# Five groups of seven in four blocks of the first gate/up products, and earlier accumulating transfers in the second's

## The chip, the cores and the metric

The kernel runs on one core of one Trainium2 chip. The core has five engines with instruction queues of their own: TensorE (PE in the profile; its weight loads are shown as PEld), VectorE (DVE), ScalarE (ACT), GpSimd (POOL) and SyncE (SP, which here only issues transfers). Sixteen DMA engines move data between the chip's memory and the core's on-chip memory. The metric is the device time of one execution in microseconds (us); less is better.

## The reference

One decoder layer in float32, on 256 tokens of 2048 features, with DeepNorm residuals:

```python
h = layer_norm(alpha * h + 0.5 * swiglu(h, w_ffn1_gu[i], w_ffn1_down[i]), ln_g[i, 0], ln_b[i, 0])
...
mixed = (jax.nn.sigmoid(gate_r) * ret_branch + jax.nn.sigmoid(gate_a) * att_branch) @ w_mix_out[i]
h = layer_norm(alpha * h + mixed, ln_g[i, 1], ln_b[i, 1])
h = layer_norm(alpha * h + 0.5 * swiglu(h, w_ffn2_gu[i], w_ffn2_down[i]), ln_g[i, 2], ln_b[i, 2])
ple = jax.nn.sigmoid(h @ w_ple_gate[i]) * (p[i] @ w_ple_proj[i])
h = layer_norm(alpha * h + ple, ln_g[i, 3], ln_b[i, 3])

def swiglu(x, w_gu, w_down):
    g, u = jnp.split(x @ w_gu, 2, axis=-1)
    return (jax.nn.silu(g) * u) @ w_down
```

The two swiglu halves, here f1 and f2, are the part that the change touches. `w_gu` is 2048 x 11264 (gate and up, 5632 columns each), `w_down` 5632 x 2048.

## The kernel before

**Precision.** TensorE multiplies in a reduced format, so each float32 operand is split into a high part (`hi`, a cast) and a low part (`lo`, raw minus `hi`). A product is three matmuls: L510 (low part of the tokens with high of the weights), L511 (high with high) and L512 (high of the tokens with low of the weights). In tile names `rf_gu` is a raw weight chunk as loaded, `hf_gu` its high part, `lf_gu` its low part; the two numbers behind them are gate or up (0 or 1) and the pair.

**Blocks.** The gate/up product of a half goes over 11 blocks (0 to 10) of 512 columns of gate and 512 of up. A block runs through 8 pairs of the inner dimension (256 rows each), in an order given by a string with one letter a pair. Each pair has a gate chunk and an up chunk of 128x1024 (512 KB). The letters:

- P: two plain chunks (`Single`). ScalarE casts (L162), VectorE subtracts (L164), TensorE does 12 matmuls for each chunk.
- F: the gate chunk is plain; the up chunk is *folded* (told below); 12 matmuls for each chunk as well.
- S: a group of seven (`Seven`): the two chunks are combined in Strassen's way, into 7 products of 3 matmuls, 21 in place of 24. VectorE forms sums and low parts in eight operations (L279, L280, L285, L287, L289, L294, L296, L298: five of 128x512, three of 128x1024), ScalarE four casts (L277, L278, L284, L293). The combined chunks are `uf`, `vf`, `bf`, with `huf`, `luf`, `hvf`, `lvf` as their parts. TensorE reads `lvf` last.
- D: a group of seven for f2 whose parts were prepared earlier and are loaded back.

The folded chunk in full: L181 (ScalarE) writes minus the raw chunk, rounded as the high part is, into the low part's slot; L182 is a DMA from GpSimd's queue that accumulates the raw chunk onto it, which leaves the low part; L198 casts the high part. VectorE has nothing to do for such a chunk; the accumulation runs on the DMA engines. The class `Folding` is its beginning (load, L181, L182), `Folded` its end (L198 and the matmuls).

In f1 blocks 1 to 10 are FFSSFSSP, with the groups on pairs 0 to 3. In f2 block 9 is FSSFSSSP, with a fifth group on pair 4 (`SEVEN_MORE`); the others of f2 mix S, D, F and P.

**The order of the work.** A list `plan` holds the units (chunks and groups) in the order in which TensorE needs them. Every unit is loaded, made and multiplied in that order; loads run ahead on SyncE's queue as far as 46 slots of on-chip memory and a budget of units allow, and the making on ScalarE and VectorE runs ahead of TensorE. `fold_at` (L201) puts a `Folding` into the plan ahead of its `Folded`: it goes back until the units passed hold `ahead` matmuls (12 a chunk, 21 a group, none for the beginning of a folded chunk); if a group of seven is near, it goes on to stand right before one. With `ahead` 0 it stands right before its `Folded`. The table `FOLD_AHEAD` (L42) gives `ahead` for each product, `FIVE` (L53) names the blocks with a fifth group.

**The end of a block.** The groups of a block share four extra PSUM banks (`f1Ns` and `f2Ns` for block N, as tiles in the profile). When the last group is done, `seven_common` folds them: ScalarE copies one bank (L634), VectorE adds the rest (L635, L637, L638, L639). Then VectorE adds the banks of gate and up (four times L1101), ScalarE applies SiLU, VectorE multiplies (L1104). These are woven between operations of the next block's groups. The result is turned for the down product: ScalarE copies it (L227), a DMA transpose is issued on SyncE (L231), ScalarE joins the halves (L238).

**In block 0** of each half, sums of the tokens for the groups are formed and split once for the whole half (L588 to L591, L113, L114), and stay in slots of their own.

Of the kernel before, what the change touches and what calls it, by code (L numbers as in the profile page):

```python
# [38 lines left out]
SLOTS = 46  # L39


FOLD_AHEAD = {"f1_gu": 34, "f1_down": 12, "f2_gu": 0, "f2_down": 12}  # L42

SEVEN = (0, 1, 2, 3)

# [4 lines left out]

ASIDE_TO = 8

FIVE = {"f1": (), "f2": (9,)}  # L53

DELAY = {"f1": 2, "f2": 1}

# [14 lines left out]
def layer(ctx: ExitStack, tc: tile.TileContext, io):  # L71
# [16 lines left out]
    def slot(shape, dt, name):  # L88
        return slots.tile(shape, dt, tag="slot", name=name)
# [111 lines left out]
    def fold_at(ahead, key):  # L201

        begun = Folding(key)
        at, time = len(plan), 0
        while at > 0 and time < ahead:
            at -= 1
            time += plan[at].time
        if ahead and any(isinstance(u, Seven) for u in plan[at - 12 : at + 1]):
            while not isinstance(plan[at], Seven):
                at -= 1  # L210
        plan.insert(at, begun)
        plan.append(Folded(begun))
# [319 lines left out]
    def block_units(units, keys):  # L532

        for kind, p in units:
            if kind == "P":
                plan.extend(Single(keys(n, p)) for n in range(2))
            elif kind == "F":
                plan.append(Single(keys(0, p)))
                fold_at(FOLD_AHEAD[keys(1, p)[0]], keys(1, p))
            else:  # L540
# [59 lines left out]
    def seven_forms(full, hi, lo, between=None):  # L600

        raw = forms_sums(full)
        if between is not None:
            between()
        return forms_split(raw, hi, lo)
# [13 lines left out]
    def units_of(order, sevens, ahead=()):  # L619

        sevens, ahead = list(sevens), list(ahead)
        plain = [p for p in range(KD // 2) if p not in sevens + ahead]
        of = {"S": sevens, "D": ahead, "P": plain, "F": plain}
        return [(kind, of[kind].pop(0)) for kind in order]
# [399 lines left out]
    def gu_units(name, j):  # L1024
        if j == 0:
            return [("P", p) for p in range(KD // 2)]
        if name == "f2" and j in AHEAD:
# [3 lines left out]
            return units_of(*((f"P{plain}SDSDSP", SEVEN[:3]) if j % 2 else (f"P{plain}SSDSSP", SEVEN)), AHEAD[j])  # L1031
        if j in FIVE[name]:
            return units_of("FSSFSSSP", SEVEN + (SEVEN_MORE,))
# [31 lines left out]
    def ffn(name, i, ht, norm, keep, residual, keepers, away):  # L1065
# [61 lines left out]
        for j in range(KF // 4):  # L1127
# [22 lines left out]
            def before(u, j=j, offset=KD // 2 - len(units)):  # L1150
# [7 lines left out]
                if j == 0 and u == 7:  # L1158
                    for g in sorted({p // 2 for p in SEVEN}):
                        hi, lo = (slot([P, 8, P], F32R, f"{name}f{w}{g}") for w in "hl")  # L1160
                        made[g] = seven_forms(keep[g], hi, lo)
                    if FIVE["f1"] and name == "f1":
                        both = slot([P, 2, 4, P], F32R, "f1fm")
# [905 lines left out]
```

## Time and profile before

| | us |
|---|---|
| runs, median of 3 | 2228.23 (2227.85 to 2229.13) |
| profiled execution | 2227.33 |
| its span | 2225.5 |
| TensorE busy in the span | 2214.5 |
| VectorE busy | 1996.5 |
| ScalarE busy | 1452.4 |
| granted TensorE clock | 0.999 of full speed |

A row of the timeline shows start, duration, engine, line, operation and tiles, and in brackets the time for which the engine stood idle before it, with what ended that. A matmul shows 0.39 us, but matmuls are pipelined and start 0.23 us apart; VectorE's operations likewise start sooner after one another than their durations say. So work is counted here from start to start. Time in a waits row is: total, times, longest.

### The profile page before, as it was taken

How to read it: one execution, taken by the hardware profiler on the slowest of the kernel's cores; microseconds unless marked ns; L12 is line 12 of the kernel's file. 1: busy time of each engine (PE TensorE's matmuls, PEld its weight loads, DVE VectorE, ACT ScalarE, POOL GpSimd, SP SyncE). 2: the span in 40 equal slices, each digit the busy share in tenths (PEclk: the TensorE clock that was granted, in tenths of full speed). 3: DMA queues.
4: the chain of work that ended last, by engine and by line, in shares of the span. 5: the costliest groups of instructions: out<-in, count | busy, mean ns of one | idle time of the engine just before them, and what ended most of it. 6: DMA issues, size and time to landing. Idle time of an engine off the chain costs nothing.

```text
span 2225.5 us, 29118 instructions
## 1 busy us (share of the span) xinstructions
PE 2214.5 (100%) x10125; PEld 1836.3 (83%) x10125; DVE 1996.5 (90%) x2654; ACT 1452.4 (65%) x1687; POOL 51.0 (2%) x65
## 2 busy tenths in 40 slices
PE   9999999999999999999999999999999999999998
PEld 8888888888888888888788888888888878888887
DVE  6989989989988889789999888779999999899887
ACT  6877777776565545557866567466767678765553
POOL 0000000000000000000000000000000000000000
PEclk9999999999999999999999999999999999999999
DMA  9998998977686889846976578888899899777871
GB/s 312 279 267 243 248 278 229 257 222 249 219 307 235 302 280 330 273 170 226 294 231 234 172 219 319 307 302 265 293 310 312 289 261 276 213 237 238 290 284 68
DMA packets 303771, 575.49 MB, mean 259 GB/s; under 512 B 98812, under 2 KB 103804, under 8 KB 303624
## 3 DMA queue, kind: packets, MB, share of 16 engines
q1 hardware_dynamic: 293576, 541.70, 73.0%
q0 software_dynamic: 8064, 29.36, 7.0%
q10 hardware_dynamic: 1984, 2.58, 0.3%
q8 instruction: 79, 1.29, 0.2%
q14 instruction: 68, 0.56, 0.1%
HBM read 490.20 MB, written 33.55 MB: 235 GB/s over the span
## 4 chain that ended last, share of the span: by engine, by line
PE 95%; DMA 2%; DVE 1%; issue 1%; ACT 0%; ACTq 0%; SPq 0%; DVEq 0%; POOLq 0%
PE f1g L510 3%; PE f1g L512 3%; PE f1g L511 3%; PE rqk L461 3%; PE f1u L510 2%; PE f1u L511 2%; PE f1u L512 2%; PE f2g L512 2%; PE f2g L510 2%; PE f2g L511 2%; PE f2u L512 2%; PE f2u L510 2%; PE f2u L511 2%; PE aqk L461 2%; PE f2e L512 1%; PE f2e L511 1%
## 5 line engine op out<-in xcount | busy, mean ns | idle before, releaser
L164 DVE TENSOR_TENSOR lf_gu<-rf_gu,hf_gu 128x1024 fp32r<-128x1024 f32 x126 | 150.0, 1227 | 29.7 <-ACT hf_gu L162 28.9
L164 DVE TENSOR_TENSOR lw_in_f<-rw_in_f,hw_in_f 128x1024 fp32r<-128x1024 f32 x132 | 158.3, 1221 | 13.6 <-ACT hw_in_f L162 13.5
L162 ACT CAST hf_gu<-rf_gu 128x1024 fp32r<-128x1024 f32 x126 | 127.7, 1050 | 37.6 <-DMA rf_gu<-in_f_gu 31.3
L162 ACT CAST hw_in_f<-rw_in_f 128x1024 fp32r<-128x1024 f32 x132 | 132.9, 1052 | 6.6 <-DMA rw_in_f<-in_w_in_f 3.8
L164 DVE TENSOR_TENSOR lf_down<-rf_down,hf_down 128x1024 fp32r<-128x1024 f32 x96 | 115.9, 1224 | 19.5 <-ACT hf_down L162 16.7
L293 ACT CAST hvf_gu<-vf_gu 128x1024 fp32r<-128x1024 f32 x80 | 84.5, 1056 | 68.7 <-DVE vf_gu L289 65.1
L284 ACT CAST huf_gu<-uf_gu 128x1024 fp32r<-128x1024 f32 x80 | 84.4, 1055 | 65.1 <-DVE uf_gu L280 62.8
L162 ACT CAST hf_down<-rf_down 128x1024 fp32r<-128x1024 f32 x96 | 98.7, 1050 | 25.4 <-DMA rf_down<-in_f_down 12.0
L287 DVE TENSOR_TENSOR lf_gu<-rf_gu,hf_gu 128x1024 fp32r<-128x1024 f32 x80 | 98.1, 1227 | 0.3
L298 DVE TENSOR_TENSOR lvf_gu<-vf_gu,hvf_gu 128x1024 fp32r<-128x1024 f32 x80 | 98.3, 1229 | 0.0
L296 DVE TENSOR_TENSOR luf_gu<-uf_gu,huf_gu 128x1024 fp32r<-128x1024 f32 x80 | 98.3, 1228 | 0.0
L510 PE MATMUL f1g<-hf_gu,xt 128*128 128x512 f32 x232 | 90.5, 390 | 0.4 <-ACT hf_gu L113 0.4
L512 PE MATMUL f1g<-lf_gu,xt 128*128 128x512 f32 x232 | 90.4, 390 | 0.0
L511 PE MATMUL f1g<-hf_gu,xt 128*128 128x512 f32 x232 | 90.3, 389 | 0.0
L277 ACT CAST hf_gu<-rf_gu 128x1024 fp32r<-128x1024 f32 x80 | 83.8, 1048 | 4.6 <-DMA rf_gu<-in_f_gu 4.6
L510 PE MATMUL f2g<-hf_gu,ht 128*128 128x512 f32 x196 | 76.4, 390 | 0.0
L512 PE MATMUL f2g<-lf_gu,ht 128*128 128x512 f32 x196 | 76.3, 389 | 0.0
L511 PE MATMUL f2g<-hf_gu,ht 128*128 128x512 f32 x196 | 76.2, 389 | 0.0
L510 PE MATMUL f1u<-hf_gu,xt 128*128 128x512 f32 x192 | 74.7, 389 | 0.0
L511 PE MATMUL f1u<-hf_gu,xt 128*128 128x512 f32 x192 | 74.7, 389 | 0.0
L512 PE MATMUL f1u<-lf_gu,xt 128*128 128x512 f32 x192 | 74.7, 389 | 0.0
L182 POOL DMA_DIRECT2D lf_gu<-rf_gu x40 | 34.8, 870 | 1632.5 <-PE f2g L511 991.6
(1546 smaller groups left out, 7205.6 us busy)
## 6 DMA issues: line engine op xcount, KB each, us to landing
rf_gu<-in_f_gu SPq DMA_DIRECT2D x362, 512.0 KB
rf_down<-in_f_down SPq DMA_DIRECT2D x176, 512.0 KB
rw_in_f<-in_w_in_f SPq DMA_DIRECT2D x148, 512.0 KB
lf_gu<-rf_gu POOLq DMA_DIRECT2D x40, 512.0 KB, 8.3
rw_rv<-in_w_rv SPq DMA_DIRECT2D x32, 512.0 KB
rw_ret<-in_w_ret SPq DMA_DIRECT2D x32, 512.0 KB
rw_mix<-in_w_mix SPq DMA_DIRECT2D x32, 512.0 KB
rw_pg<-in_w_pg SPq DMA_DIRECT2D x32, 512.0 KB
```

The source lines that it names most:

```text
L162: act.copy(c.hi, c.raw)
L164: dve.tensor_tensor(c.lo, c.raw, c.hi, ALU.subtract)
L277: act.copy(a.hi, a.raw)
L284: act.copy(uh, u)
L287: dve.tensor_tensor(a.lo, a.raw, a.hi, ALU.subtract)
L293: act.copy(vh, v)
L296: dve.tensor_tensor(ul, u, uh, ALU.subtract)
L298: dve.tensor_tensor(vl, v, vh, ALU.subtract)
L461: pe.matmul(ps[f], hi[:, kk, f * P : (f + 1) * P], rhs(k), start=k == 0, stop=k == n_k - 1,)
L510: pe.matmul(o, al, bh, start=first, stop=False)
L511: pe.matmul(o, ah, bh, start=False, stop=False)
L512: pe.matmul(o, ah, bl, start=False, stop=self.left == 0)
```

## The change

Two tables are changed.

```diff
-FOLD_AHEAD = {"f1_gu": 34, "f1_down": 12, "f2_gu": 0, "f2_down": 12}
+FOLD_AHEAD = {"f1_gu": 34, "f1_down": 12, "f2_gu": 12, "f2_down": 12}
...
-FIVE = {"f1": (), "f2": (9,)}
+FIVE = {"f1": (3, 5, 7, 9), "f2": (9,)}
```

With `FIVE["f1"]`, blocks 3, 5, 7 and 9 of f1 become FSSFSSSP: pair 4, an F before, is a fifth group. Its token sums (`f1fm`, high and low part in one slot) are formed in block 0 by the lines that the kernel had for it already. The program has 12 matmuls fewer (9930 rows on TensorE for 9942), 33 operations more on VectorE (2625 for 2592), 5 more on ScalarE, and four accumulating transfers fewer on GpSimd (66 rows for 70).

TensorE at the end of f1's block 3. The last pair ahead of the closing P is the group on pair 3 before; in the change a group on pair 4 stands behind it. Before:

```order
L510 MATMUL f1g_1212<-hvf_gu_0_3_1446,xt 128x512
L511 MATMUL f1g_1212<-hvf_gu_0_3_1446,xt 128x512
L512 MATMUL f1g_1212<-lvf_gu_0_3_1447,xt 128x512
L510 MATMUL f1g_1211<-hf_gu_0_7_1466,xt 128x512
L511 MATMUL f1g_1211<-hf_gu_0_7_1466,xt 128x512
```

In the change, the end of the group on pair 4 (its first product with `lvf` is the third row):

```order
L510 MATMUL f13s_1303<-hvf_gu_0_4_1452,f1fm 128x512
L511 MATMUL f13s_1303<-hvf_gu_0_4_1452,f1fm 128x512
L512 MATMUL f13s_1303<-lvf_gu_0_4_1453,f1fm 128x512
...
L510 MATMUL f1g_1236<-hvf_gu_0_4_1452,xt 128x512
L511 MATMUL f1g_1236<-hvf_gu_0_4_1452,xt 128x512
L512 MATMUL f1g_1236<-lvf_gu_0_4_1453,xt 128x512
L510 MATMUL f1g_1235<-hf_gu_0_7_1483,xt 128x512
```

TensorE's closing P (pair 7) now follows the group on pair 4, where it followed the one on pair 3.

VectorE ahead of the fold of block 3 (L635 on `f13s`). Before, three subtractions of plain chunks stand between the group on pair 3 and the fold:

```order
L298 TENSOR_TENSOR lvf_gu_0_3_1447<-vf_gu_0_3_1432,hvf_gu_0_3_1446 128x1024
L164 TENSOR_TENSOR lf_gu_0_7_1467<-rf_gu_0_7_1365,hf_gu_0_7_1466 128x1024
L164 TENSOR_TENSOR lf_gu_1_7_1492<-rf_gu_1_7_1411,hf_gu_1_7_1491 128x1024
L164 TENSOR_TENSOR lf_gu_0_4_1519<-rf_gu_0_4_1452,hf_gu_0_4_1518 128x1024
L635 TENSOR_TENSOR evw<-eve,f13s_1339 128x512
```

In the change:

```order
L298 TENSOR_TENSOR lvf_gu_0_3_1412<-vf_gu_0_3_1397,hvf_gu_0_3_1411 128x1024
L279 TENSOR_TENSOR uf_gu_0_4_1437<-rf_gu_1_4_1335 128x512
L280 TENSOR_TENSOR uf_gu_0_4_1437<-rf_gu_0_4_1333,rf_gu_1_4_1335 128x512
L285 TENSOR_TENSOR vf_gu_0_4_1438<-rf_gu_0_4_1333,uf_gu_0_4_1437 128x512
L287 TENSOR_TENSOR lf_gu_0_4_1441<-rf_gu_0_4_1333,hf_gu_0_4_1440 128x1024
L289 TENSOR_TENSOR vf_gu_0_4_1438<-vf_gu_0_4_1438,rf_gu_0_4_1333 128x512
L294 TENSOR_TENSOR bf_gu_0_4_1439<-rf_gu_1_4_1335,bf_gu_0_4_1439 128x512
L296 TENSOR_TENSOR luf_gu_0_4_1447<-uf_gu_0_4_1437,huf_gu_0_4_1446 128x1024
L298 TENSOR_TENSOR lvf_gu_0_4_1453<-vf_gu_0_4_1438,hvf_gu_0_4_1452 128x1024
L164 TENSOR_TENSOR lf_gu_0_7_1484<-rf_gu_0_7_1382,hf_gu_0_7_1483 128x1024
```

Eight operations more stand ahead of the fold; one L164 earlier in the block (the plain chunk of the F that went) is gone.

With `FOLD_AHEAD["f2_gu"]` at 12, each folded chunk of f2's blocks 4 to 10 is begun earlier. SyncE's queue around the end of f2's block 7 (pairs 3 and 7 are that block's; pairs 5, 6 and 0 are block 8's; the transpose is of block 6's result). Before:

```order
L127 DMA rf_gu_0_3_15834<-in_f_gu 128x2x512
L127 DMA rf_gu_1_3_15836<-in_f_gu 128x2x512
L127 DMA rf_gu_0_7_15883<-in_f_gu 128x2x512
L127 DMA rf_gu_1_7_15885<-in_f_gu 128x2x512
L127 DMA rf_gu_0_5_15887<-in_f_gu 128x2x512
L127 DMA rf_gu_1_5_15914<-in_f_gu 128x2x512
L231 DMA_TRANSPOSE mf_15916<-wf_15870 128x16x128
L127 DMA rf_gu_0_6_15943<-in_f_gu 128x2x512
L127 DMA rf_gu_1_6_15945<-in_f_gu 128x2x512
L127 DMA rf_gu_0_0_15976<-in_f_gu 128x2x512
```

In the change:

```order
L127 DMA rf_gu_1_6_15878<-in_f_gu 128x2x512
L127 DMA rf_gu_0_3_15880<-in_f_gu 128x2x512
L127 DMA rf_gu_1_3_15882<-in_f_gu 128x2x512
L127 DMA rf_gu_0_7_15884<-in_f_gu 128x2x512
L127 DMA rf_gu_1_7_15934<-in_f_gu 128x2x512
L127 DMA rf_gu_0_5_15936<-in_f_gu 128x2x512
L127 DMA rf_gu_1_5_15963<-in_f_gu 128x2x512
L231 DMA_TRANSPOSE mf_15965<-wf_15921 128x16x128
L127 DMA rf_gu_0_6_15992<-in_f_gu 128x2x512
L127 DMA rf_gu_0_0_16023<-in_f_gu 128x2x512
```

Block 8's chunk 1_6 moved from behind the transpose to ahead of both chunks of block 7's group on pair 3. ScalarE's L181 on it and GpSimd's L182 move with it: L181 stands ahead of that group's first cast (L277), where it stood ahead of L198 on the same chunk. The order on VectorE in f2 does not change.

In f1's blocks 3, 5, 7 and 9 the transposes on SyncE stand one load later in the queue than before, and on VectorE the rest of the fold of the block before (L637 to L639) is woven into the first group, its gating (L1101, L1104) into the second, where they stood ahead of and in the first.

## The prediction

> **What bounds the kernel now.** I read the shares first, then the chain of waits, then TensorE's waits, then the blocks of the two feed-forward halves one by one.
>
> ```profile
> PE 2214.5 (100%) x10125; PEld 1836.3 (83%) x10125; DVE 1996.5 (90%) x2654; ACT 1452.4 (65%) x1687; POOL 51.0 (2%) x65
> PE 95%; DMA 2%; DVE 1%; issue 1%; ACT 0%; ACTq 0%; SPq 0%; DVEq 0%; POOLq 0%
> PE f2u L512 <- DMA lf_gu<-rf_gu: 1.8, 3, 1.1
> 123.60:164.40 40.80, 40.80 (x182) 33.80 (x181) 37.45 (x46) 30.85 (x34) 2.60 (x3) 1.00 0.95 257
> 1761.82:1802.53 40.71, 40.45 (x178) 33.12 (x177) 38.73 (x49) 28.02 (x32) 0.86 (x1) 1.00 0.98 303
> 1802.53:1845.21 42.68, 41.03 (x178) 32.87 (x178) 42.55 (x54) 31.22 (x35) 1.72 (x2) 1.00 0.88 250
> ```
>
> TensorE sets the end: 95% of the chain. Its waits on anything in the feed-forward halves are three, 1.8 us together, all in f2, on accumulating transfers. The last three rows are one block each (columns: length, then busy time of PE, PE's loads, VectorE, ScalarE, GpSimd; clock; DMA share). The first is an f1 block of four groups of seven: 4x21 + 4x24 = 180 matmuls in 40.80 us, so **0.2267 us a matmul** at clock 1.00 (182 is the 180 and those cut by the window's ends). The next two are blocks 8 and 9 of f2, with five groups (5x21 + 3x24 = 177, which at that pace is 40.12 us): 40.71 and 42.68, so f2 loses 0.6 and 2.6 us there. VectorE is busy 37.45 of 40.80 in the f1 block, 42.55 of 42.68 in the five-group block 9. VectorE is the second bound, and this change loads it.
>
> **f1, what is removed.** Blocks 3, 5, 7 and 9 go from FFSSFSSP to FSSFSSSP: pair 4 becomes a group of seven, 21 matmuls for 24. 4 x 3 x 0.2267 = **2.72 us** off a TensorE that waits for nothing there. The program has 12 matmuls fewer, so that much is sure if nothing else waits. One accumulating transfer in each of the four blocks goes too.
>
> **f1, what is added.** VectorE gets eight operations for one subtraction. Their starts, from the one kind of block that is already FSSFSSSP (f2's ninth), last group:
>
> ```profile
> 1805.86 0.69 DVE L635 TENSOR_TENSOR evw<-eve,f28s 128x512 f32<-128x512 f32 x1
> ...
> 1838.58 0.70 DVE L279 TENSOR_TENSOR uf_gu<-rf_gu 128x512 f32<-128x512 f32 x1
> 1839.18 0.70 DVE L280 TENSOR_TENSOR uf_gu<-rf_gu,rf_gu 128x512 f32<-128x512 f32 x1
> 1839.78 0.70 DVE L285 TENSOR_TENSOR vf_gu<-rf_gu,uf_gu 128x512 f32<-128x512 f32 x1
> 1840.38 1.23 DVE L287 TENSOR_TENSOR lf_gu<-rf_gu,hf_gu 128x1024 fp32r<-128x1024 f32 x1
> 1841.52 0.70 DVE L289 TENSOR_TENSOR vf_gu<-vf_gu,rf_gu 128x512 f32<-128x512 f32 x1
> ...
> 1843.85 1.24 DVE L298 TENSOR_TENSOR lvf_gu<-vf_gu,hvf_gu 128x1024 fp32r<-128x1024 f32 x1
> 1844.99 3.51 DVE L164 TENSOR_TENSOR lf_gu<-rf_gu,hf_gu 128x1024 fp32r<-128x1024 f32 x3
> 1848.62 0.69 DVE L635 TENSOR_TENSOR evw<-eve,f29s 128x512 f32<-128x512 f32 x1
> ```
>
> An operation of 512 columns takes its place for 0.60 us, one of 1024 for 1.14. A group is 1844.99 - 1838.58 = 6.41 us, against 1.14 for the subtraction it replaces: 5.27 us more for VectorE in a block in which TensorE needs 0.68 less. The whole block is 1848.62 - 1805.86 = **42.76 us** of VectorE, against 40.12 of TensorE. So VectorE falls 2.64 us behind in each five-group block. Four-group blocks stand between them, where it idles:
>
> ```profile
> 163.94 0.39 PE L512 MATMUL f13s<-lvf_gu,f1fh 128*128 128x512 f32 x1
> 164.44 0.69 DVE L635 TENSOR_TENSOR evw<-eve,f13s 128x512 f32<-128x512 f32 x1 [3.25 <-PE f13s L512]
> 369.48 0.69 DVE L635 TENSOR_TENSOR evw<-eve,f18s 128x512 f32<-128x512 f32 x1 [0.21 <-PE f1g L511]
> 287.77 0.69 DVE L635 TENSOR_TENSOR evw<-eve,f16s 128x512 f32<-128x512 f32 x1 [0.21 <-ACT eve L634]
> 286.33 1.23 DVE L164 TENSOR_TENSOR lf_gu<-rf_gu,hf_gu 128x1024 fp32r<-128x1024 f32 x1 [2.69 <-ACT hf_gu L162]
> 366.24 1.23 DVE L164 TENSOR_TENSOR lf_gu<-rf_gu,hf_gu 128x1024 fp32r<-128x1024 f32 x1 [3.33 <-ACT hf_gu L162]
> 408.04 1.23 DVE L164 TENSOR_TENSOR lf_gu<-rf_gu,hf_gu 128x1024 fp32r<-128x1024 f32 x1 [3.27 <-ACT hf_gu L162]
> ```
>
> 3.25 us idle at a block's end pays for 2.64, with 0.6 over. What is late next is the fifth group itself. From the block's first fold (L635) to the end of its last subtraction VectorE needs 1845.09 (1843.85 + 1.24) - 1805.86 = 39.23 us. TensorE reads that result 0.50 us ahead of the next fold (163.94 and 164.44), at 40.12 - 0.50 = 39.62. Lead: **0.4 us**. The folds of blocks 6 and 8 start at 287.77 and 369.48, where 164.44 + 3 or 5 x 40.80 would put them at 286.84 and 368.44: 0.9 and 1.0 us late, since a chunk came late (2.69 and 3.33 idle). Blocks 7 and 9, then, start with a deficit of 0.5 to 0.6. Stalls at those two groups: between 0 (the dropped accumulation gives the loads room) and 0.6 each. I take 0.5 us in all. The gating of the block before (L1101) also moves behind the first group, as it stands in f2's block 9:
>
> ```profile
> 1820.01 0.69 DVE L1101 TENSOR_TENSOR evw<-evw,f2u 128x512 f32<-128x512 f32 x1
> 1820.84 0.47 PE L510 MATMUL f29s<-hvf_gu,f2fl 128*128 128x512 f32 x1
> ```
>
> There TensorE's matmul comes 0.14 us after the fourth L1101 ends (1820.01 + 0.69): it waited for the bank, a few tenths at most. But that block's fold began 1805.86 - 1802.53 = 3.33 us after TensorE's last read of a `lvf`, in f1 it is 0.50: 2.8 us more of room, so no wait in f1. The four small operations and the split that build the extra operand in block 0 are at most 5 x 0.69 = 3.4 us of VectorE, once; the 3.25 us idle ahead of an early fold swallows them, and they cost 3.4 at most without it. ScalarE (30.85 of 40.80) and SyncE's transposes, one load later in these blocks, I cost at nothing: the joined activations are not read before f1's down products; without that cover it is one load. The extra operand also holds one of the kernel's 46 slots until block 9, so a load that waits for a slot can come one load later; that I leave to rival (b). What a load costs is read from the DMA rows:
>
> ```profile
> GB/s 366 264 148 280 239 255 330 371 109 235 241 208 312 370 114 187 296 234 234 375 291 148 271 246 233 328 356 39 282 289 203 308 387 148 136 314 228 265 361 313
> q0 software_dynamic: 2733, 9.96, 20.0%
> lf_gu<-rf_gu POOLq DMA_DIRECT2D x40, 512.0 KB, 8.3
> ```
>
> 512 KB at the highest slice, 387 GB/s, is 1.35 us. The second row (the window 160 to 420, 19 accumulations) is 0.2 x 260 / 19 = 2.7 us of all 16 engines for one accumulation, so each five-group block frees 2.7 us of DMA. f1: -2.72 + 0.5 = -2.2.
>
> **f2, what moves.** In blocks 4 to 10 the load, negation and accumulation of a folded chunk go ahead of the group before it (4.76 us of TensorE) or of 12 matmuls (2.72). The largest of the waits:
>
> ```profile
> 1823.50 0.86 POOL L182 DMA_DIRECT2D lf_gu<-rf_gu  x1 [17.87 <-ACT lf_gu L181]
> 1830.03 0.39 PE L511 MATMUL f2u<-hf_gu,ht 128*128 128x512 f32 x1
> 1831.48 0.50 PE L512 MATMUL f2u<-lf_gu,ht 128*128 128x512 f32 x1 [1.06 <-DMA lf_gu<-rf_gu]
> 1831.82 0.40 PE L510 MATMUL f2u<-hf_gu,ht 128*128 128x512 f32 x1
> ```
>
> Issued at 1823.50 and awaited at 1830.26, it landed near 1831.4, 7.9 us after issue. Begun 2.7 to 4.8 us sooner it lands ahead of need: the 1.8 us of waits go, and with what is lost around them (1831.48 - 1830.03 - 0.23 = 1.22, and 0.11 at the row after, for a wait of 1.06) some 2.3. But TensorE then meets VectorE:
>
> ```profile
> 1754.55 0.69 DVE L279 TENSOR_TENSOR uf_gu<-rf_gu 128x512 f32<-128x512 f32 x1 [2.08 <-PE f27s L512]
> 1756.98 1.04 ACT L227 COPY wf<-evw 128x1024 uint16<-128x1024 uint16 x1
> 1759.84 1.22 DVE L298 TENSOR_TENSOR lvf_gu<-vf_gu,hvf_gu 128x1024 fp32r<-128x1024 f32 x1
> 1761.82 0.39 PE L512 MATMUL f27s<-lvf_gu,f2fh 128*128 128x512 f32 x1
> 1767.35 1.23 DVE L164 TENSOR_TENSOR lf_gu<-rf_gu,hf_gu 128x1024 fp32r<-128x1024 f32 x1 [0.36 <-ACT hf_gu L162]
> 1771.29 0.69 DVE L279 TENSOR_TENSOR uf_gu<-rf_gu 128x512 f32<-128x512 f32 x1 [1.51 <-DMA rf_gu<-in_f_gu]
> 1801.08 1.24 DVE L298 TENSOR_TENSOR lvf_gu<-vf_gu,hvf_gu 128x1024 fp32r<-128x1024 f32 x1
> 1802.53 0.40 PE L512 MATMUL f28s<-lvf_gu,f2fh 128*128 128x512 f32 x1
> 1845.21 0.43 PE L512 MATMUL f29s<-lvf_gu,f2f2h 128*128 128x512 f32 x1
> ```
>
> From 1771.29 VectorE has no idle row to the end of block 9. Its last group of block 8 is ready at 1802.32 and read at 1802.53 (0.21 lead); of block 9, ready 1845.09, read 1845.21 (0.12). TensorE freed from the transfers would wait for these rows instead: what is won is how much sooner VectorE's run at 1771.29 starts, and the 0.1 of lead. That start waits for a load (1.51 idle). Block 8's load of chunk 1_6 leaves the queue ahead of it: one load, 1.35 us, sooner. But it now stands ahead of the two chunks of block 7's last group (1754.55), which waits for them: that group starts 1.35 later, ready at 1762.4 for 1761.82, a new stall of 0.6 in block 7, and ScalarE's copy at 1756.98, in line behind it, is later too. The transpose waits for that copy, and SyncE has the loads in question queued behind the transpose: the 1.35 is given back. The run starts near where it did; 0.36 + 1.51 of idle absorb VectorE's own 1.35. Bounds: 2.3 won, if the start moves that far; 1.4 lost, if the accumulation's 2.7 us fall on the loads behind the transpose. I take **-0.1**, by the two leads.
>
> By the Trainium skill, DMA: Bandwidth & Descriptors, "Anatomy of one DMA — SWDGE (gpsimd) path", a GpSimd-issued transfer takes about 2.0 us plus its bytes at 436 GB/s, an estimate of 3.2 us here. It would have landed at 1826.7, TensorE would not have waited, and f2's edit would bring 0 and the sum would be -2.2. The trace disagrees: 7.9 us at this row, 8.3 median, so that result gets no chance.
>
> **Sum.** 2227.33 (the profiled execution; span 2225.5) - 2.72 + 0.5 - 0.1 = 2225.0. The median of the runs is 0.90 higher: **2225.9 us**.
>
> **Rivals.** (a) *f2's waits are won in full.* For: VectorE's start at 1771.29 hangs on one load. Against: leads of 0.21 and 0.12. -2.72 - 2.3 = -5.0, from the median some 2223.2. (b) *Slower: VectorE's lag meets late chunks in f1.* Place: the fifth group of blocks 7 and 9; it decides once a five-group block's first fold is over 0.4 us late. In block 9 the chunk subtracted at 408.04 had been waited for 3.27 us; its transfer landed near 406.9 (a cast of 1.05 ahead), that of the new fifth group one load before, 405.6; with 6.5 us of group it is ready at 412.1, where TensorE wants it at 369.48 + 39.62 = 409.1: 3.0. With 0.6 in block 7, +0.9 net, 2229.1; with the 2.64 lag carried on top, +3.5, 2231.7. Against: the block's DMA is 2.7 us lighter. (c) *The change brings fewer matmuls but no time*: each fifth group stalls about what it saves (0.68), as f2's ninth block did (42.68 for 177 matmuls, where f1's blocks of four groups take 40.80 for 180): from the median, 2228.23 - 0.1, about 2228.1.
>
> **Chances.** Forecast 0.48, (a) 0.15, (b) 0.20, (c) 0.17. Range 2223.0 to 2230.3: from (a), through (c), to the nearer half of (b). 0.2%, about what a measurement of this kernel can tell from no change, is 4.46 us: faster means under 2223.8, slower over 2232.7. Faster: most of (a) and the low edge of the forecast, 0.16. Slower: (b) with f2's 1.4 lost on top, 0.09. Same: 0.75.
>
> **What would show it.** f1: five-group blocks of 40.1 us, fold to fold of VectorE 42.8 there and some 38 in the next; TensorE waits at most 0.6 for L298's result, in blocks 7 and 9. More than 1 us there, or the chunk waits of 3.3 us grown, is (b); 0.7 in all four is (c). f2: no wait on an accumulating transfer, and in their place waits on L298's results in blocks 7 (0.6), 8 and 9; if these three blocks run through at 0.2267 a matmul, it is (a). The forecast is wrong where block 8's first group starts on VectorE over 1 us sooner or later (beside f1's gain) than at 1771.29, or where blocks 3 and 5 already stall.

## The result: slower by 0.14%, and the profile after

| | before | change |
|---|---|---|
| runs, median of 20 each | 2227.56 us | 2230.72 us |
| profiled execution, span | 2225.5 us | 2229.1 us |
| VectorE busy in it | 1996.5 us | 2017.4 us |

The ratio is 1.0014, with a 95% interval of 1.0008 to 1.0020. The forecast was 2225.9 us in a range of 2223.0 to 2230.3: wrong, and on the wrong side. Rival (b) comes nearest, with the loss in f2 on top of it. The page of the changed kernel, its engines and its chain of waits:

```profile
PE 2216.5 (99%) x10113; PEld 1832.9 (82%) x10113; DVE 2017.4 (90%) x2687; ACT 1453.2 (65%) x1692; POOL 47.4 (2%) x61
PE 77%; DVE 7%; issue 2%; ACT 1%; DMA 1%; SPq 0%; ACTq 0%; DVEq 0%
```

TensorE fell from 95% of the chain to 77%, VectorE rose from 1% to 7%. TensorE's waits (total, times, longest) say on what:

```profile
PE f19s L512 <- DVE luf_gu L296: 0.7, 1, 0.7
PE f29s L512 <- DVE luf_gu L296: 0.7, 1, 0.7
PE f1d L512 <- DVE lf_down L164: 0.5, 1, 0.5
PE f27s L510 <- DVE evw L1101: 0.4, 2, 0.3
PE f19s L510 <- DVE evw L1101: 0.3, 1, 0.3
PE f15s L512 <- DVE luf_gu L296: 0.2, 1, 0.2
```

The three waits on accumulating transfers are gone, as the change meant. The waits in the two halves are now on VectorE, the largest in f1's blocks 5 and 9, in f1's down products, and in f2's blocks 7 and 9. By blocks of f1 (from TensorE's last product of one block's groups to that of the next: 3 to 10):

```profile
124.17:164.29 40.12, 40.12 (x178) 33.22 (x177) 40.12 (x52) 29.68 (x33) 2.61 (x3) 1.00 0.76 210
164.29:205.09 40.80, 40.80 (x181) 33.78 (x180) 38.77 (x49) 31.31 (x35) 1.72 (x2) 1.00 0.93 270
205.09:246.20 41.11, 40.70 (x179) 33.06 (x177) 41.11 (x52) 30.68 (x34) 2.58 (x3) 1.00 0.84 246
246.20:287.04 40.84, 40.84 (x182) 33.78 (x180) 40.07 (x50) 32.67 (x37) 1.73 (x2) 1.00 0.93 279
287.04:327.16 40.12, 40.12 (x179) 33.22 (x177) 40.12 (x52) 29.73 (x33) 2.58 (x3) 1.00 0.72 211
327.16:367.96 40.80, 40.80 (x182) 33.78 (x180) 38.03 (x48) 30.61 (x34) 1.72 (x2) 1.00 0.97 254
367.96:410.79 42.83, 41.39 (x179) 32.83 (x178) 41.93 (x53) 31.53 (x35) 2.61 (x3) 1.00 0.81 237
410.79:451.93 41.14, 41.08 (x181) 33.70 (x180) 38.75 (x48) 30.01 (x33) 0.86 (x1) 1.00 0.90 266
```

Blocks 3 and 7 take 40.12 us: the 0.68 is won there in full. What a block takes over its 40.12 (five groups) or 40.80 (four) is called its stall here. It is 0.99 in block 5, 2.71 in block 9 and 0.34 in block 10. The DMA share (the last number but one) is 0.72 to 0.84 in the five-group blocks and 0.90 to 0.97 in the four-group blocks. Before, f1's blocks 2 to 9 had 0.90 to 0.97 as well, so the dropped transfers make the five-group blocks lighter and leave the blocks behind them as full as they were. Block 9's stall, TensorE's waits on the gating of block 8, then VectorE's rows and TensorE's at the fifth group:

```profile
381.54 0.47 PE L510 MATMUL f19s<-hf_gu,xt 128*128 128x512 f32 x1 [0.28 <-DVE eve L1101]
385.68 0.47 PE L510 MATMUL f19s<-hvf_gu,f1fl 128*128 128x512 f32 x1 [0.32 <-DVE evw L1101]
...
407.57 1.22 DVE L296 TENSOR_TENSOR luf_gu<-uf_gu,huf_gu 128x1024 fp32r<-128x1024 f32 x1
408.70 1.22 DVE L298 TENSOR_TENSOR lvf_gu<-vf_gu,hvf_gu 128x1024 fp32r<-128x1024 f32 x1
...
408.85 0.50 PE L512 MATMUL f19s<-luf_gu,f1fm 128*128 128x512 f32 x1 [0.67 <-DVE luf_gu L296]
409.98 0.50 PE L512 MATMUL f19s<-lvf_gu,f1fm 128*128 128x512 f32 x1 [0.17 <-DVE lvf_gu L298]
```

TensorE takes the fifth group's parts the moment that VectorE has made them. Counted from start to start, TensorE loses 1.4 us at the fifth group and 1.2 around the two waits on L1101. VectorE's folds and its idle time ahead of work:

```profile
123.97 0.69 DVE L635 TENSOR_TENSOR evw<-eve,f12s 128x512 f32<-128x512 f32 x1 [0.61 <-issue]
166.53 0.68 DVE L635 TENSOR_TENSOR evw<-eve,f13s 128x512 f32<-128x512 f32 x1
172.36 0.69 DVE L279 TENSOR_TENSOR uf_gu<-rf_gu 128x512 f32<-128x512 f32 x1 [1.81 <-DMA rf_gu<-in_f_gu]
206.10 0.68 DVE L635 TENSOR_TENSOR evw<-eve,f14s 128x512 f32<-128x512 f32 x1
286.85 0.69 DVE L635 TENSOR_TENSOR evw<-eve,f16s 128x512 f32<-128x512 f32 x1 [0.66 <-PE f16s L512]
331.81 1.23 DVE L164 TENSOR_TENSOR lf_gu<-rf_gu,hf_gu 128x1024 fp32r<-128x1024 f32 x1 [0.93 <-ACT hf_gu L162]
335.97 0.69 DVE L279 TENSOR_TENSOR uf_gu<-rf_gu 128x512 f32<-128x512 f32 x1 [1.73 <-DMA rf_gu<-in_f_gu]
369.71 0.68 DVE L635 TENSOR_TENSOR evw<-eve,f18s 128x512 f32<-128x512 f32 x1
371.29 0.69 DVE L279 TENSOR_TENSOR uf_gu<-rf_gu 128x512 f32<-128x512 f32 x1 [0.90 <-DMA rf_gu<-in_f_gu]
```

Block 3 costs VectorE 166.53 - 123.97 = 42.56 us (forecast 42.76). The four-group block behind it was to cost some 38 and costs 206.10 - 166.53 = 39.57, since VectorE stands 1.81 us idle ahead of its first group, for a load. Blocks 3 and 4 together take 82.13 us of VectorE and 80.92 of TensorE, so VectorE comes out of them 1.2 us further behind TensorE; this is called its lag. Block 6 has no such wait: at its end VectorE is level again (it waits 0.66 us for TensorE at 286.85), and block 7 doesn't stall. In block 8 it stands idle for 0.93 + 1.73 us, and its fold (369.71) starts 1.75 us after TensorE's last product (367.96), where a level one starts 0.2 us ahead. Block 9 then adds a late load of its own, 0.90 us.

### The profile page after: what moved, and what is told of

It is laid out like the page before. It is cut to its first block, busy times and chain, and to the rows that moved or that the text cites. A ratio compares the mean times of both kernels' runs of the same rounds, so it can differ in the third digit from the quotient of the medians.

```text
span 2229.1 us, 29157 instructions
## 1 busy us (share of the span) xinstructions
PE 2216.5 (99%) x10113; PEld 1832.9 (82%) x10113; DVE 2017.4 (90%) x2687; ACT 1453.2 (65%) x1692; POOL 47.4 (2%) x61
## 4 chain that ended last, share of the span: by engine, by line
PE 77%; DVE 7%; issue 2%; ACT 1%; DMA 1%; SPq 0%; ACTq 0%; DVEq 0%
PE rqk L461 3%; PE f2g L510 2%; PE f2g L511 2%; PE f2g L512 2%; PE f2u L511 2%; PE f2u L510 2%; PE f2u L512 2%; PE aqk L461 2%; PE f1e L512 1%; PE f2d L510 1%; PE f2d L512 1%; PE f1e L511 1%; PE f1e L510 1%; PE f2d L511 1%; PE gt L510 1%
## 5 line engine op out<-in xcount | busy, mean ns | idle before, releaser
L164 DVE TENSOR_TENSOR lw_in_f<-rw_in_f,hw_in_f 128x1024 fp32r<-128x1024 f32 x132 | 158.2, 1219 | 14.1 <-ACT hw_in_f L162 14.0
L164 DVE TENSOR_TENSOR lf_gu<-rf_gu,hf_gu 128x1024 fp32r<-128x1024 f32 x122 | 144.4, 1221 | 24.3 <-ACT hf_gu L162 23.3
L164 DVE TENSOR_TENSOR lf_down<-rf_down,hf_down 128x1024 fp32r<-128x1024 f32 x96 | 115.5, 1222 | 17.5 <-ACT hf_down L162 13.1
L277 ACT CAST hf_gu<-rf_gu 128x1024 fp32r<-128x1024 f32 x84 | 87.8, 1045 | 1.8 <-DMA rf_gu<-in_f_gu 1.8
L510 PE MATMUL f1g<-hf_gu,xt 128*128 128x512 f32 x220 | 86.1, 391 | 0.0
L512 PE MATMUL f1g<-lf_gu,xt 128*128 128x512 f32 x220 | 85.8, 390 | 0.0
L511 PE MATMUL f1g<-hf_gu,xt 128*128 128x512 f32 x220 | 85.8, 390 | 0.0
L510 PE MATMUL f1u<-hf_gu,xt 128*128 128x512 f32 x176 | 68.5, 389 | 0.0
L511 PE MATMUL f1u<-hf_gu,xt 128*128 128x512 f32 x176 | 68.5, 389 | 0.0
L512 PE MATMUL f1u<-lf_gu,xt 128*128 128x512 f32 x176 | 68.5, 389 | 0.0
L279 DVE TENSOR_TENSOR uf_gu<-rf_gu 128x512 f32<-128x512 f32 x84 | 57.6, 686 | 10.1 <-DMA rf_gu<-in_f_gu 10.0
```

Of the source, the lines that this page charges most:

```text
L164: dve.tensor_tensor(c.lo, c.raw, c.hi, ALU.subtract)
L277: act.copy(a.hi, a.raw)
L510: pe.matmul(o, al, bh, start=first, stop=False)
L511: pe.matmul(o, ah, bh, start=False, stop=False)
L512: pe.matmul(o, ah, bl, start=False, stop=self.left == 0)
```

## The experiments

Where time was lost is read from the traces: how much later TensorE ends a part than in the profiled execution of the kernel before. "f1" is what blocks 3 to 10 of f1 add, "down" what f1's down products add, "f2" what blocks 5 to 10 of f2 add. The whole times stand beside the kernel before on the same chip.

| kernel | f1 | down | f2 | median, before | ratio, 95% |
|---|---|---|---|---|---|
| the change | +1.39 | +0.82 | +1.48 | 2230.72, 2227.56 | 1.0014 (1.0008 to 1.0020) |
| e1 f1 only | +1.18 | +0.79 | -0.44 | 2228.57, 2226.78 | 1.0006 (0.9998 to 1.0015) |
| e2 f2 only | 0 | 0 | +2.22 | 2228.61, 2226.78 | 1.0003 (0.9994 to 1.0012) |
| e3 f2, ahead of the chunk | 0 | 0 | -0.52 | 2227.58, 2226.78 | 0.9999 (0.9990 to 1.0008) |
| e4 operand formed, unused | 0 | 0 | -0.23 | 2228.17, 2226.78 | 1.0007 (0.9998 to 1.0016) |
| e5 blocks 3, 7 | -1.36 | 0 | +0.36 | 2226.37, 2226.99 | 0.9997 (0.9988 to 1.0006) |
| e6 blocks 3, 6, 9 | +0.03 | +0.79 | -0.54 | 2227.56, 2226.99 | 1.0013 (0.9997 to 1.0030) |
| e7 plain pair 5 | -2.14 | 0 | +1.10 | 2224.20, 2226.99 | 0.9991 (0.9982 to 1.0000) |
| e8 folded pair 7 | +1.05 | 0 | -0.69 | 2227.19, 2226.99 | 0.9999 (0.9990 to 1.0008) |
| e9 e7 with e3 | -1.10 | 0 | -0.16 | 2224.67, 2226.93 | 0.9987 (0.9979 to 0.9995) |
| e10 f2, load alone | 0 | 0 | +0.05 | 2228.08, 2226.93 | 1.0004 (0.9993 to 1.0015) |
| e11 e7 again | -2.00 | 0 | -1.59 | 2224.97, 2226.70 | 0.9991 (0.9983 to 1.0000) |
| e12 e9 again | -1.40 | 0 | -0.21 | 2224.67, 2226.70 | 0.9990 (0.9981 to 0.9999) |
| e13 e1, 32 slots | -0.24 | +0.82 | -0.12 | 2228.23, 2227.01 | 1.0012 (1.0003 to 1.0021) |
| e14 e9, 32 slots | -2.21 | 0 | -0.54 | 2224.20, 2227.01 | 0.9993 (0.9984 to 1.0002) |
| e15 e1, transpose early | -2.36 | +0.14 | +0.13 | 2224.05, 2226.88 | 0.9988 (0.9979 to 0.9997) |
| e16 e9, transpose early | -0.42 | +0.12 | -0.79 | 2225.21, 2226.88 | 0.9993 (0.9984 to 1.0002) |
| e17 change, transpose early | -2.72 | +0.03 | +2.55 | 2226.05, 2226.91 | 0.9992 (0.9984 to 1.0001) |
| e18 e15 with e3 | -2.72 | 0 | +0.69 | 2224.67, 2226.91 | 0.9989 (0.9980 to 0.9998) |

f1's column is repeatable to some tenths in e7 and e11. f2's is not: with f2's code as it was, it spans -1.59 to +1.10. The stretch between the halves, which no run changed, spans -1.3 to +0.6 as well, so a median can differ from what f1 and f2 add. Every row of f1, down and f2 is one execution; the intervals of most versions hold 1, and e4, which lost next to nothing in its trace, stands at 1.0007. So the parts are read from the traces, and the whole times serve only where two intervals lie apart.

**Which half loses.** e1 has the change's `FIVE` and `"f2_gu": 0`, e2 has the change's `FOLD_AHEAD` and `"f1": ()`.

> Only the five-group blocks in f1; f2's folding as before. Theory (VectorE's lag of 2.64 us after a five-group block is not repaid in the next block when its loads come late, so the fifth group of a later block stalls): TensorE reaches the end of f1's gate/up part 1.7 us later than in the kernel before, and f2 takes as long as before; whole kernel +1.5 to +2.5 us. Rival (f2's edit carries the whole loss): f1's part 2.2 us shorter, kernel -2 us.

> Only the earlier folding in f2; f1 as before. Theory (the folded chunk's load ahead of a group's two chunks delays that group on VectorE, and VectorE sets f2's end): f2's gate/up part 1.0 to 1.5 us longer than before, no waits on accumulating transfers, waits on L1101, L296 and L298 in their place. Rival (f2's loss in the whole change comes from f1's later end and its slots): f2 0 to 0.5 us shorter.

Both lose in their traces, each by itself: e1 +1.18 and +0.79 in f1, which repeats the change's +1.39 and +0.82, and e2 +2.22 in f2, twice the highest that f2 adds with its code as it was (+1.10). Both are 1.8 us slower by the medians, but the intervals hold 1. The theory holds in kind in both. In size, e1's end of gate/up is 1.83 us later for the 1.7 expected, 0.65 of it lost ahead of block 2 already; e2's 2.22 lies over the 1.0 to 1.5 expected.

**f2: the place of the load.** e3 keeps the folded chunk ahead of the chunk before it, but not ahead of a group:

```diff
-        if ahead and any(isinstance(u, Seven) for u in plan[at - 12 : at + 1]):
+        if ahead and key[0] != "f2_gu" and any(isinstance(u, Seven) for u in plan[at - 12 : at + 1]):
```

> Only f2, and each folded chunk begins ahead of the chunk before it (its own pair's gate chunk, 12 matmuls) but not ahead of a group of seven. Theory (the harm is the load ahead of the group's loads): no group of block 7 starts later on VectorE, the fold waits shrink by 2.7 us of lead, and f2 is within 0.4 us of before. Rival (the harm is the accumulation running earlier against the loads behind the transpose): f2 about 1 us longer, as with the whole edit.

e10 moves the load alone. The folded chunk's beginning is split in two, a unit that only loads, where the change puts it, and one that negates and accumulates, right ahead of the high cast:

```diff
...
+        if key[0] == "f2_gu":
+            begun = Reading(key)
+            late = FoldingLate(begun)
+            plan.insert(at, begun)
+            plan.append(late)
+            plan.append(Folded(late))
+            return
```

> f1 as before. In f2 the folded chunk's load stands where the change puts it, ahead of a group's two loads, but its negation (L181) and accumulation (L182) stay right ahead of its high cast, as before. Theory (the load's place in the queue alone delays the group): VectorE's last group of block 7 starts a load, 1.3 us, later, as with the whole edit, and TensorE loses 1 us or more by the end of block 7. Rival (the negation ahead of the group's first cast on ScalarE, or the accumulation running against loads, does the harm): block 7 as before, within 0.3 us.

VectorE's last group of f2's block 3 (the row near 1594) and first group of block 4 (near 1610), before, in e2 and in e10 (where L315 is the line L279):

```profile
1593.24 0.69 DVE L279 TENSOR_TENSOR uf_gu<-rf_gu 128x512 f32<-128x512 f32 x1 [0.27 <-DMA rf_gu<-in_f_gu]
1609.54 0.69 DVE L279 TENSOR_TENSOR uf_gu<-rf_gu 128x512 f32<-128x512 f32 x1 [1.53 <-DMA rf_gu<-in_f_gu]
```

```profile
1595.15 0.69 DVE L279 TENSOR_TENSOR uf_gu<-rf_gu 128x512 f32<-128x512 f32 x1 [2.31 <-DMA rf_gu<-in_f_gu]
1609.25 1.23 DVE L164 TENSOR_TENSOR lf_gu<-rf_gu,hf_gu 128x1024 fp32r<-128x1024 f32 x1 [1.66 <-ACT hf_gu L162]
1611.59 0.68 DVE L279 TENSOR_TENSOR uf_gu<-rf_gu 128x512 f32<-128x512 f32 x1
```

```profile
1595.69 0.69 DVE L315 TENSOR_TENSOR uf_gu<-rf_gu 128x512 f32<-128x512 f32 x1 [2.17 <-DMA rf_gu<-in_f_gu]
1610.39 0.68 DVE L315 TENSOR_TENSOR uf_gu<-rf_gu 128x512 f32<-128x512 f32 x1
```

Taken against each run's own start of f2 (e2 0.1 sooner, e10 0.6 later than before), the group of block 3 starts 2.0 us later in e2 and 1.9 in e10: the load's place does that alone, as the theory had it. But by block 4's first group e10 is 0.3 late, and e2 still 2.1: the idle that was to absorb the lateness does so only where the accumulation isn't in flight. In e2 the accumulation was in flight from 1593.9 to 1602.8. The transpose, issued at 1598.7 (2.0 later than before), held SyncE's queue for 4.02 us in place of 1.88 before and 1.90 in e10, and SyncE issued the next load at 1602.8, where it was 1598.7 before. The same is seen at the ends of blocks 5 and 7: in all three traces with this edit (the change, e2, e17) the transposes there and at the end of block 3 hold the queue for 4.0 to 5.6 us with an accumulation in flight, before and in e10 for 1.9 to 2.9 with none. So neither theory was right alone: the load delays the group, the accumulation and the transpose keep it delayed. e10 also keeps the negation on ScalarE (L181) in its old place; its part isn't separated from the accumulation's. TensorE lost 0.47 us in block 7 with the load alone, not the 1 us expected, and nothing by the end. e3, with neither ahead of a group, removes the three waits on transfers and lost nothing; whether it wins cannot be told, as its -0.52 is inside the spread of f2 (and e18, with the same f2, gave 0.69 back).

**The operand of block 0.** e4 forms it and doesn't use it (the fifth groups are f2's alone).

> The extra operand of f1's fifth groups is formed in block 0 and keeps its slot, but no block uses it; f2 as before. Theory (the six operations in block 0 push block 1's last group, and the slot matters little): the stall of some 0.55 us at the end of block 1 stays, no other stall appears in f1, kernel +0.5 us. Rival (the slot held is what makes loads late in the four-group blocks): late loads of 1.7 us ahead of blocks' first groups and +1 us or more.

TensorE lost 0.23 us at the end of block 1, then nothing in f1. The slot that the operand holds costs TensorE nothing by itself.

**f1: does the lag come from VectorE's work or from late loads?** e5 and e6 change only the set of blocks, to `(3, 7)` and `(3, 6, 9)`.

> Fifth groups only in f1's blocks 3 and 7; f2 as before. Theory (the lag of one five-group block is repaid if more than one four-group block follows): no stall in blocks 7 and 9, 2 x 0.68 = 1.36 us saved by the end of gate/up, less 0.2 to 0.6 at the end of block 1; no wait in f1's down products; end of gate/up 0.8 to 1.2 us sooner. Rival (each fifth group after the first stalls): end of gate/up 0 to 1 us later.

> Fifth groups in f1's blocks 3, 6 and 9, two blocks of four between them. Theory: blocks 6 and 9 start repaid, 3 x 0.68 = 2.04 us saved there, less 0.2 to 0.6 in block 1 and 0.3 to 1.2 in block 10 and the down products behind block 9: 0.5 to 1.3 us sooner at the end of f1's part. Rival (the stall belongs to the fifth group itself): 1 us or more of stall in blocks 6 and 9, later than before.

e5 wins 2 x 0.68 = 1.36 us exactly, with no stall. In e6 blocks 3 and 6 win theirs, and block 6's lag is repaid over two blocks, as the theory had it; but block 9 stalls 1.65 us all the same, as the rival had it for blocks 6 and 9, and the down products lose 0.79. VectorE's two waits ahead of that:

```profile
367.91 0.69 DVE L635 TENSOR_TENSOR evw<-eve,f18s 128x512 f32<-128x512 f32 x1 [0.36 <-PE f18s L512]
370.38 0.69 DVE L279 TENSOR_TENSOR uf_gu<-rf_gu 128x512 f32<-128x512 f32 x1 [1.78 <-DMA rf_gu<-in_f_gu]
```

At the end of block 8 VectorE waits for TensorE, so it is level; then block 9's own first group waits 1.78 us for a load, in a block that has no idle time to give. So here a late load stalls a fifth group with no lag carried in.

e7 makes pair 5 plain in the block behind each five-group block: more work for VectorE, one accumulation fewer.

```diff
-        order = "FFSSFSSP" if name == "f1" or j > 8 else "PFSSFSSP"
+        order = "FPSSFSSP" if name == "f1" and j - 1 in FIVE["f1"] else "FFSSFSSP" if name == "f1" or j > 8 else "PFSSFSSP"
```

> Fifth groups in blocks 3, 5, 7 and 9; in blocks 4, 6, 8 and 10 pair 5 is plain (FPSSFSSP), so that its accumulation is not in flight at the start of the block and VectorE does one subtraction (1.14 us) more. Theory (the late loads at those blocks' first groups come from accumulations and the transpose in flight with them): the idle of 1.8 us ahead of the first group shrinks to under 0.7, block 9's stall halves, end of gate/up 0.5 to 1.5 us sooner than with the four blocks alone. Rival (VectorE's work alone decides): 1.14 more a pair of blocks, stalls 1 us longer each, end of gate/up 2 us or more later than with the four blocks alone.

e8 goes the other way: less work for VectorE, one accumulation more.

```diff
-            return units_of("FSSFSSSP", SEVEN + (SEVEN_MORE,))
+            return units_of("FSSFSSSF" if name == "f1" else "FSSFSSSP", SEVEN + (SEVEN_MORE,))
```

> Fifth groups in blocks 3, 5, 7 and 9, whose last pair is folded (FSSFSSSF): VectorE does one subtraction (1.14 us) less in each, the DMA engines one accumulation (2.7 us) more. Rival of the run before (VectorE's work decides): lag 1.5 us in place of 2.64, no stall in block 9 beyond 0.5, end of gate/up 1.5 us sooner than before. Theory (late loads decide as much): the accumulations in flight at the next block's start are one more, its first group comes a further 1 us late or more, and the stalls of blocks 5 and 9 stay at 1 us or above.

VectorE's folds around e7's block 4, and e8's last wait ahead of the fold of block 7:

```profile
166.25 0.71 DVE L635 TENSOR_TENSOR evw<-eve,f13s 128x512 f32<-128x512 f32 x1
204.86 0.69 DVE L635 TENSOR_TENSOR evw<-eve,f14s 128x512 f32<-128x512 f32 x1
```

```profile
333.34 1.23 DVE L164 TENSOR_TENSOR lf_gu<-rf_gu,hf_gu 128x1024 fp32r<-128x1024 f32 x1 [4.32 <-ACT hf_gu L162]
```

With 1.14 us more of work e7's block 4 costs VectorE 38.61 us, 0.96 less than the change's, as no load is waited for. f1 wins 2.14 (2.00 in e11). e8's VectorE has less to do and waits more; blocks 5 and 9 stall 0.99 and 2.4 us. VectorE's work alone does not decide.

e9 puts e7 and e3 together. It won 1.10 us in f1 and 0.16 in f2, 2.3 us by the medians, where 2.5 to 3.5 had been expected. Repeated, e7 came to 1.7 us (e11, 2 to 3 expected) and e9 to 2.0 (e12, 2 to 3.5 expected).

**What makes the loads late.** In the trace of the change, SyncE issues no load from 145.4 to 153.6 us. By the waits of SyncE's queue such loads wait for TensorE, which still reads the slot that they are to fill (6.9 us the longest there); from 150 to 154 the DMA engines stand idle (busy tenths of the 20 us from 150, in 40 slices):

```profile
DMA  0000000008699999997989989999696999998998
```

Then come that load, the transpose, two accumulations (issued at 156.37 and 157.31) and the loads of block 4's start, up to 166.52. e13 gives f1 two slots more in the budget (`slots_for_weights(32)` for 30).

> The four five-group blocks alone, as in the first run, but f1's blocks may hold 32 slots of weights in place of 30. In the trace of the change the issue of loads stands still from 145.4 to 153.6 in block 3, and the DMA engines with it, before the late loads of block 4. Theory A (a group takes 6 or 7 slots, so the fifth group stops the loads for want of room, and what was not loaded then comes late): the standstill shrinks, the idle ahead of block 4's first group falls under 0.7 us, blocks 5 and 9 stall half as much or less, end of gate/up 1 us or more sooner than with 30. Theory B (the two accumulations and the transpose in flight are enough to make them late): the late loads stay, end of gate/up within 0.7 us of that with 30.

The standstill stayed (147.1 to 155.3), the idle ahead of block 4's first group too (1.66 us). Theory A's cure fails; that no slot at all would shorten the standstill isn't shown. f1's -0.24 is better than e1's +1.18, with the end at the same time, as this execution lost 1.3 us more than e1's ahead of block 2. e14 puts the two slots into the best version so far.

> FPSSFSSP behind the five-group blocks, f2's chunk-only folding, and 32 slots. Theory A: block 9's stall goes too, f1 2.0 to 2.7 us sooner than before, kernel 3 us faster than before. Theory B: as without the two slots, 2 to 2.5 us faster than before.

f1 gave -2.21 there, for -1.10 and -1.40 without, and the kernel 2.8 us by the medians: between the two theories, and the interval holds 1.

e15 keeps the four five-group blocks and moves f1's transposes: `DELAY = {"f1": 1, "f2": 1}` for 2 in f1. In block 3 the transpose then stands ahead of the load that is held up, not behind it. The same number moves ScalarE's joins (L238) one unit earlier. In the change they run at 172.94 and 176.45, behind the late load (awaited until 172.36), so they are not what made it late.

> The four five-group blocks alone, as in the first run, but f1's transposes go one unit earlier (DELAY 1 in place of 2), so that in the five-group blocks the transpose stands ahead of the load that is held up, in a stretch in which the DMA engines are idle, and not behind it. Theory C (the transpose, in flight with the two accumulations, makes the loads late): the transpose is over before 158, the idle ahead of block 4's first group falls from 1.8 to under 0.8 us, blocks 5 and 9 stall half as much. Theory B' (the two accumulations and the held-up loads are enough): idle ahead of block 4's first group 1.3 us or more, stalls as before.

SyncE's queue around it, before, in the change and in e15:

```profile
140.71 6.77 SPq L231 DMA_TRANSPOSE mf<-wf  x1
147.59 12.11 SPq L127 DMA_DIRECT2D rf_gu<-in_f_gu  x7
```

```profile
154.07 3.58 SPq L231 DMA_TRANSPOSE mf<-wf  x1
157.76 7.44 SPq L127 DMA_DIRECT2D rf_gu<-in_f_gu  x6
```

```profile
147.54 2.89 SPq L231 DMA_TRANSPOSE mf<-wf  x1
154.09 6.67 SPq L127 DMA_DIRECT2D rf_gu<-in_f_gu  x5
```

And VectorE in e15:

```profile
166.80 0.68 DVE L635 TENSOR_TENSOR evw<-eve,f13s 128x512 f32<-128x512 f32 x1
171.06 0.69 DVE L279 TENSOR_TENSOR uf_gu<-rf_gu 128x512 f32<-128x512 f32 x1 [0.45 <-DMA rf_gu<-in_f_gu]
205.17 0.69 DVE L635 TENSOR_TENSOR evw<-eve,f14s 128x512 f32<-128x512 f32 x1 [0.29 <-PE f14s L512]
```

In the change the transpose takes SyncE's queue from 154.07 to 157.65, with the loads of block 4's start behind it; in e15 it runs in the gap, the held-up load is issued at 154.09, and the loads behind it from 156.13 on, where the change has 157.76. The idle ahead of block 4's first group falls from 1.81 to 0.45 us, VectorE waits for TensorE again at the block's end, and f1 wins 2.36 us. Block 5 stalls no more, block 9 0.33. Theory C holds for the transpose's place. Whether it does its harm by holding SyncE's queue or by taking the DMA engines' time beside the accumulations isn't separated. e16 to e18 put the earlier transposes on other versions.

> The best version (FPSSFSSP behind the five-group blocks, f2's chunk-only folding) with f1's transposes one unit earlier. Theory C: block 9's stall goes, kernel 0.5 to 1.5 us faster than without it. Theory B': no difference beyond 0.5 us.

> The change as it is, both edits, with f1's transposes one unit earlier (DELAY 1). Theory (f1's loss is the transpose's place, f2's loss is its own): end of f1's gate/up 1.2 us or more sooner than before, f2's gate/up still 1 us or more longer than before, kernel within 1 us of before. Rival (f2's loss came with f1's late end): kernel 2 us faster than before or better.

> The four five-group blocks, f1's transposes one unit earlier, and f2's folded chunks begun ahead of their own gate chunk only. Theory: f1 1.5 us or more sooner, f2 no longer than before; kernel 2.5 to 3.5 us faster than before. Rival (f2 is set by VectorE's run and an earlier start brings nothing): 2 us faster or less.

In e17 and e18 f1 wins 2.72 us, all of the 12 matmuls. In e17 f2 loses 2.55 although f1 ended early: f2's loss is its own. The whole times bear the transpose's part out: the intervals of e1 and e15 lie apart, and so do those of the change and e17. e18 is 2.2 us faster than before, not the 2.5 to 3.5 expected; f2 gave 0.69 back. In e16, with pair 5 plain as well, theory C's forecast failed: VectorE waited 1.77 us for a load ahead of block 9's first group (1.11 in e9, 0.77 in e12), block 9 stalled again, and f1 won 0.42 only. The two cures don't add; what makes that load late stays open. Of the versions that beat both kernels e15 is the simplest: 2.8 us by the medians, ratio 0.9988 (0.9979 to 0.9997). e7, e9, e11, e12, e14 and e18 can't be told apart from it.

## Why the prediction was wrong

- **f1's removal (2.72)**: right. Blocks 3 and 7 take the forecast 40.12 us, and e17 and e18 show all four.
- **VectorE's cost of a five-group block**: right, 42.56 us for 42.76.
- **"3.25 us idle at a block's end pays for 2.64"**: the step that failed. I carried over the idle time of a four-group block as it stood in the trace before, where no block of five stands ahead of it. In blocks 4 and 8 of the change 1.8 and 2.7 us of it (1.81; 0.93 + 1.73) stand at the block's start, where loads are awaited, and can't be used to catch up. Only in block 6 did it pay as forecast. Blocks 5 and 9 stalled 0.99 and 2.71 us where 0.5 in all was forecast, at blocks 7 and 9.
- **"SyncE's transposes, one load later in these blocks, I cost at nothing"**: this is where the idle of block 4 came from: in e15, with the transposes earlier, it shrinks to 0.45 us, and in e15, e17 and e18 f1's loss turns into 2.36 to 2.72 us won. I asked who reads the transpose's result, and named one load as the price. I didn't ask what stands behind it on its queue, and that the one load now ahead of it was itself held up for a slot (153.6). The transpose then fell on the accumulations and on block 4's loads.
- **Rival (b)** named one place right, and its sign: block 9's first fold (369.71) was 1.75 us behind TensorE, over its 0.4. That its 3.0 lies near the measured 2.71 is luck. It put all of it at the fifth group, where 1.4 us was lost; 1.2 was lost around L1101, which the prediction had excluded. It expected 0.6 in block 7, where nothing was lost, and left out block 5. Its cause was the late chunk of the old trace, with "the block's DMA is 2.7 us lighter" against it. That didn't help: the five-group block's DMA is lighter (share 0.72 to 0.84), but the next block's is not.
- **The operand in block 0, at nothing**: small, and not nothing. TensorE lost 0.23 us at the end of block 1 in e4, 0.5 in e5.
- **L1101, "no wait in f1"**: right for blocks 3, 5 and 7. In block 9, with a lag of 1.95 us carried in, two waits of 0.28 and 0.32 us stand there, 1.2 us with what is lost around them.
- **f1's down products**: not in the sum. The lag ran on through block 10, whose fold starts 6.33 us after TensorE's last product (3.31 before), and a subtraction (L164) came late: 0.82 us. Where it starts 5.64 after (e15), 0.14 is lost; at 5.35 (e7), nothing.
- **f2, -0.1**: mis-sized, and its mechanism was half right. The three waits on transfers went and VectorE took their place, as forecast. But the row that was to start near 1771.29, or sooner by what f1 won, started later. The forecast had 0.36 + 1.51 us of idle absorb VectorE's 1.35:

```profile
1758.05 2.82 SPq L231 DMA_TRANSPOSE mf<-wf  x1
```

```profile
1757.19 0.87 POOL L182 DMA_DIRECT2D lf_gu<-rf_gu  x1 [38.55 <-ACT lf_gu L181]
1761.91 4.32 SPq L231 DMA_TRANSPOSE mf<-wf  x1
1774.88 0.68 DVE L279 TENSOR_TENSOR uf_gu<-rf_gu 128x512 f32<-128x512 f32 x1
```

  The first row is the transpose before; the others are of the change. TensorE came to f2 1.9 us later than before, and the row at 1774.88 is 3.6 later: 1.7 us of loss. The bound of 1.4 ("if the accumulation's 2.7 us fall on the loads behind the transpose") was the case that came: the accumulation issued at 1757.19 landed at 1766.37, the transpose held the queue until 1766.23, and the loads behind it came 5.4 us later than before, at 1766.33. The measured f2 was +1.48, and +2.22 and +2.55 in e2 and e17. The same happens from block 3 on, where I had looked at blocks 7 to 9 only.
- **The range**: it held (b) to its nearer half and left out f2's loss on top of it, which had 0.09. Both losses are of one kind, transfers that are brought together at a block's seam, though each came without the other (e1, e2) and f1's cure left f2's loss as it was (e17).

## What to carry to other kernels

A step that moves past a queue entry costs what is queued behind it, at the time when it then runs: ask of each moved transfer which entry now stands ahead of it and whether that one is held up. Idle time of an engine in an old trace is slack only where it stands; after a change it can move to the front of the stretch and be of no use. Where two edits both bring transfers to the seams of blocks, look at what each seam then has in flight before giving each edit its own small risk.

## What the runs showed of the hardware that was not expected

The time for which a DMA transpose of the same size held SyncE's queue differed widely: 1.3 to 6.6 us in f1 of the change and 4.9 to 8.8 before. At the ends of f2's blocks 3, 5 and 7 it was 1.9 to 2.9 us without an accumulation in flight and 4.0 to 5.6 us with one. Loads that stand behind it and have their slots are issued only then (157.76 behind 157.65 in the change, 147.59 behind 147.48 before). One unit's difference in its place was worth some 3.5 us of TensorE's time in f1 (+1.18 in e1, -2.36 in e15) and 4.1 with both edits (+1.39, and -2.72 in e17), but brought nothing where pair 5 is plain (-1.10 in e9, -0.42 in e16). And stretches with the same code moved by 1 to 1.6 us between executions (f2 -1.59 in e11, +1.10 in e7, with the same kernel), so a single trace doesn't settle a difference of that size.
